# A decoder block on one core: attention products ordered by the probabilities' two parts, and a cast moved to GpSimd

## The chip, the cores and the metric

The kernel runs on one core of a Trainium2 chip. The metric is device time in microseconds of one execution, as the median of several runs. The engines are TensorE (PE, and PEld for its weight loads), VectorE (DVE), ScalarE (ACT), GpSimd (POOL) and SyncE (SP), which here only issues DMAs.

## The reference

One decoder block over 1024 tokens of width 1024, in float32. Dilated attention and a convolution module run side by side on the same normalised input; gates merge them, and a SwiGLU feed-forward layer follows. What matters here is the attention: 24 heads of width 64 in three groups.

```python
DILATED_GROUPS = ((128, 1), (512, 4), (2048, 16))   # window, dilation
...
s = jnp.einsum('brnqhd,brnkhd->brnhqk', qb, kb).astype(jnp.float32) * (Dh ** -0.5) + bias
s = jnp.where(valid[:, None], s, NEG_INF)
lse = jax.nn.logsumexp(s, axis=-1)
p = jnp.exp(s - lse[..., None])
o = jnp.einsum('brnhqk,brnkhd->brnqhd', p, vb.astype(jnp.float32))
...
alpha = jax.nn.softmax(jnp.stack(lses, axis=0), axis=0)
o = jnp.einsum('gbsh,gbshd->bshd', alpha, jnp.stack(outs, axis=0))
```

The other parts are large matrix products, normalisations and a depthwise convolution of 31 taps:

```python
merged = jax.nn.sigmoid(z_ga) * y_attn + jax.nn.sigmoid(z_gc) * y_conv
x = x + rms_norm(merged @ w_mix_out[l], g_post_mix[l])
h = rms_norm(x, g_pre_ffn[l])
x = x + rms_norm(swiglu_ffn(h, w_ffn_in[l], w_ffn_out[l]), g_post_ffn[l])
```

## The kernel before

**Two parts.** An operand of a product is split into a high part, which is the number rounded to TensorE's shorter float32 form, and a low part, which is what the rounding left. A product is then high by high, high by low and low by high. Casts to the high part run on ScalarE as a rule; the subtraction that gives the low part runs on VectorE or GpSimd.

**The order of the work.** All instructions are put out by one program in a fixed order, so each engine's queue is written by hand. The main thread issues the large products. After each group of them it calls `tick`, which runs things that are due by a count of ticks (`later`), and `beat`, which advances the attention: `attention` is a generator, and each `yield` in it is a place where products of the main thread can come between. How many beats fall between the main products is set by a rate (0.42 beside the value projections, 0.8 beside the convolution's output product), so several pauses often follow one another with nothing between. While the attention runs, the main thread computes the value projections (`v`, L954 and L955, with the copies L965 and sums L976), one gate, and the first output products of the convolution (`unit`, L318 to L320, with its splits L190, L191, L1266, L1267 and the result L1613).

**The attention.** It has 96 steps: three groups of heads x 4 pairs of heads x 8 blocks of 128 queries. A pair of heads in a group is a unit of 8 steps. In step `s`:

- `att_s`: the scores of both heads (PE L1067), then their bias and minimum (DVE L1070).
- `att_e`: the exponentials of the step before (ACT L1080).
- a pause; then `added`, what the last finished pair left to do: two additions (`att_o`, DVE L1167).
- `att_t`, four steps behind: one head's probabilities for a pair of blocks are transposed (PE L1105), cast to their high part (`hi`, ACT L1112), and the low part is subtracted (`lo`, DVE L1113).
- a pause; then `att_p`, five steps behind: the values' products with `hi` (PE L1137) and with `lo` (PE L1138). The stationary operand holds, for each block of keys, 64 columns of the values' high part and then 64 of their low part; the product with `lo` uses the first 66 columns only. There are two or three blocks of keys: in the third group two of 128 queries, otherwise a first one of 256 and one or two of 128. There is a pause after the first and after the second block.

After the second head's products the lower 64 rows of the bank are copied out (ACT L1146), and the two additions in the next step add them to the upper 64 rows. When a unit is through, its output goes to memory six ticks later (SP L1173).

**The values.** `value_parts` makes a unit's stationary operand in two halves, in the unit's fourth and fifth step: the cast of the values to their high part (ACT L927) and the subtraction of it (POOL L928). The first products of the unit run in the sixth step. In the second group the even blocks lie in the first half and the odd ones in the second (`place`). In the seventh and eighth step GpSimd copies the next unit's queries within SBUF (`double`, L896 and L897). SyncE loads the next unit's queries, keys and bias (L880, L881, L887, L489) in its first steps, and its values before they are needed (L913).

Of the kernel before, what the change touches and what calls it, by code (L numbers as in the profile page):

```python
# [58 lines left out]
def f(ap):  # L59
    return ap.bitcast(F32)  # L60


class Build:
# [858 lines left out]
    def value_parts(self, x, i):  # L922

        v = self.slot(F32R)
        d = v.rearrange("p (t e c) -> p t e c", t=8, e=2)
        y = x[:, i * H:(i + 1) * H].rearrange("p (t c) -> p t c", t=8)
        self.nc.scalar.copy(d[:, :, 0], y)  # L927
        self.nc.gpsimd.tensor_tensor(d[:, :, 1], y, f(d[:, :, 0]), op=OP.subtract)  # L928
        return v

# [56 lines left out]
    def attention(self):  # L987

        live, s, total = {}, 0, 96
        order = [(g, 2 * hg + i) for hg in range(2) for g in range(3) for i in range(2)]  # L990
        nxt, cur, u, x, V = self.stacks(*order.pop(0)), None, 8, None, None
        for i in range(5):
            self.stack_load(nxt)
        second, doubled = self.stacks(*order.pop(0)), 0

        def there():
            return nxt[1] // 2 * 3 + nxt[0] < self.vn

        while s < total + self.LP:
            if s < total:  # L1000
                if x is None and nxt and there():
                    x = self.values(*nxt[:2])
                if u == 8:
                    while self.normed < 9 or x is None:
                        if second and second[5] < min(5, self.normed - 6):
                            self.stack_load(second)
                        if cur is None and doubled < min(2, self.normed - 5):
                            self.double(nxt, doubled)
                            doubled += 1
                        if x is None and there():  # L1010
                            x = self.values(*nxt[:2])
                        yield 0
                    cur, u, nxt, V = nxt, 0, None, []
                    self.ending = s == total - 8
                live[s] = a = {}
                self.att_s(a, cur, V, u)
                u += 1

                if u in (4, 5):
                    if len(V) < 2:  # L1020
                        V.append(self.value_parts(x, u - 4))
                    if u == 5:
                        x = None
                if u == 6 and cur[0] == 2:
                    self.other_stats(cur)
                if u in (6, 7) and nxt:
                    self.double(nxt, u - 6)
                if u == 8:
                    cur[2] = cur[3] = V = None
                if u == 1:  # L1030
                    if second:
                        nxt, second = second, None
                    elif order:
                        nxt = self.stacks(*order.pop(0))
                if nxt and nxt[5] < 5:
                    self.stack_load(nxt)
            if 0 <= s - 1 < total:
                self.att_e(live[s - 1])
            yield 0
            if self.added:  # L1040
                self.added()
                self.added = None
            if 0 <= s - self.LT < total:
                self.att_t(live, s - self.LT)
                yield 0
            if 0 <= s - self.LP < total:
                yield from self.att_p(live, s - self.LP)
            s += 1
        self.added()
        self.added = None  # L1050

    def att_s(self, a, p, V, u):
# [63 lines left out]
    def att_p(self, live, k):  # L1116


        nc = self.nc
        a, b, hh = live[k & ~1], live[k | 1], k & 1  # L1120
        g, hp, u = a["g"], a["hp"], a["u"]
        if hh == 0:
            a["o"] = self.bank("o")
        ps = a["o"]
        hi, lo = a.pop(("pt", hh))

        if g == 2:
            todo = [(u, 0, 128, 0), (u + 1, 128, 128, 128)]
        else:
            n = 256 + 128 * (len(a["blocks"]) > 1)  # L1130
            todo = [(u, 0, 256, 0)] + [(u - 1, 256, 128, 0)] * (n > 256) + [(u + 1, n, 128, 128)]
        for j, (kb, x, n, q) in enumerate(todo):
            kb = self.place(g, kb)
            v = a["V"][kb // 4]
            c = (kb % 4) * 256 + hh * 128
            o = ps[:, hh * 256 + q:hh * 256 + q + n]
            nc.tensor.matmul(o, v[:, c:c + 128], hi[:, x:x + n], start=j == 0, stop=False, skip_group_check=True)  # L1137
            nc.tensor.matmul(o[0:66], v[:, c:c + 66], lo[:, x:x + n], start=False, stop=j == len(todo) - 1,  # L1138
                             skip_group_check=True)
            if j < 2:  # L1140
                yield 0
        hi = lo = v = None
        if hh == 0:
            return
        low = self.half()
        nc.scalar.copy(low[0:64], ps[64:128])  # L1146
        del live[k - 1], live[k]
        self.added = lambda: self.att_o(a, ps, low)

    def att_o(self, a, ps, low):  # L1150

        nc = self.nc
        g, hp, u = a["g"], a["hp"], a["u"]
        if u == 0:
            self.O = self.ring()

        O = self.O
        e = (8, 2, 128)[g]
        if g == 0:
            d = O.rearrange("p (c m) -> p m c", c=8)[:, u * 16:u * 16 + 32]  # L1160
        elif g == 1:
            d = O.rearrange("p (e c m) -> p c m e", e=2, c=4)[:, u // 2]
        else:
            d = O[:, u * 128:u * 128 + 256].rearrange("p (c m) -> p c m", c=2)
        for h in range(2):
            x, y = (z[0:64, h * 256:(h + 1) * 256].rearrange("p (a e) -> p a e", e=e) for z in (ps, low))
            nc.vector.tensor_tensor(d[h * 64:(h + 1) * 64], x, y, op=OP.add)  # L1167
        a["o"] = None
        if u == 6:

            kept = g == 2 and hp > 1
            if not kept:
                self.later(6, lambda x=self.O: nc.sync.dma_start(self.d_att[g, hp], x))  # L1173
            if g == 2:
                self.merges.append(self.bg(self.merge(hp, a["p"][4], self.O if kept else None)))
            self.O = None
# [885 lines left out]
```

## Time and profile before

| | |
|---|---|
| median of 3 runs | 1698.06 us (1697.9 to 1698.22) |
| profiled execution | 1700.21 us |
| its span, first to last instruction | 1698.4 us |
| granted TensorE clock | 0.999 |
| attention, first scores to last product | 616 to 854 us |
| L927, cast of the values on ScalarE | 24 times, 622 ns mean |
| L928, subtraction on GpSimd | 24 times, 1289 ns mean |

In the rows that follow, an instruction is named by its line, engine and operation, then by what it writes and reads (`b`, `c`, `d` are buffers in SBUF of different sizes, `p` banks in PSUM). Behind a group stand its busy time, the mean duration in ns, and the idle time of its engine just before it with what ended that idle time. A timeline row is start, duration, engine, line, operation, and in brackets the idle time before it. The ends of products are modelled, so the distance from one start to the next says more than their duration.

### The profile page before, as it was taken

Reading aid. Unit: us, or ns where it says so; the run is one execution under the profiler, and the core shown is the slowest. Engines: PE = TensorE matmul, PEld = TensorE weight load, DVE = VectorE, ACT = ScalarE, POOL = GpSimd, SP = SyncE. Lnnn points to the kernel's source line nnn. Section 1 sums busy time; section 2 is a strip of 40 time slices with the busy share of each in tenths; the row PEclk is TensorE's granted clock in tenths of the full one; section 3 lists DMA queues with packets and bytes.
Section 4 is the critical chain, followed back from the end, with each engine's and each line's share of the span. In section 5 each row is a group of like instructions: output and inputs, shape, how many; then the busy total and the mean of one; then the engine's idle time right before and its main releaser. Section 6 shows DMA issues by size and latency. Waiting matters only on the chain.

```text
span 1698.4 us, 23450 instructions
## 1 busy us (share of the span) xinstructions
PE 1675.6 (99%) x8158; PEld 1404.2 (83%) x8158; DVE 1256.8 (74%) x2216; ACT 826.8 (49%) x1622; POOL 492.6 (29%) x369
## 2 busy tenths in 40 slices
PE   8999999999999999999899999999999999999998
PEld 6788888888888889999788888888888888888886
DVE  6789988788999767788885845775665556677686
ACT  6343434343444588888822446543333333354463
POOL 0007777888886254654200300000000000000000
PEclk9999999999999999999999999999999999999999
DMA  4252433355566987779998622132223222494234
GB/s 167 104 186 87 142 131 130 137 191 179 183 173 165 284 270 213 230 224 254 301 275 305 230 87 84 60 129 95 93 93 125 99 93 93 168 377 130 102 130 155
DMA packets 162354, 283.35 MB, mean 167 GB/s; under 512 B 47249, under 2 KB 78732, under 8 KB 162236
## 3 DMA queue, kind: packets, MB, share of 16 engines
q1 hardware_dynamic: 161516, 281.18, 50.8%
q8 instruction: 64, 1.05, 0.3%
q0 software_dynamic: 432, 0.42, 0.1%
q14 instruction: 54, 0.44, 0.1%
q10 hardware_dynamic: 288, 0.27, 0.0%
HBM read 191.10 MB, written 95.42 MB: 169 GB/s over the span
## 4 chain that ended last, share of the span: by engine, by line
PE 90%; DMA 4%; DVE 2%; ACT 1%; issue 1%; POOL 1%; SPq 0%; DVEq 0%; ACTq 0%; POOLq 0%
PE p L334 15%; PE p L335 15%; PE p L336 15%; PE p L1946 12%; PE p L1675 5%; PE p L954 5%; PE p L318 5%; PE p L319 5%; PE p L320 5%; PE p L955 2%; PE p L1067 2%; PE p L1105 1%; DMA b<-dq 1%; PE p L1138 1%; PE p L1137 1%
## 5 line engine op out<-in xcount | busy, mean ns | idle before, releaser
L334 PE MATMUL p<-b,b 128*128 128x512 f32 x1204 | 468.7, 389 | 0.4 <-ACT c L353 0.3
L336 PE MATMUL p<-b,b 128*128 128x512 f32 x1204 | 468.4, 389 | 0.0
L335 PE MATMUL p<-b,b 128*128 128x512 f32 x1204 | 468.4, 389 | 0.0
L334 PEld LDWEIGHTS p<-b,b 128*128 128x128 f32 x1204 | 226.0, 188 | 48.4 <-DVE c L850 1.0
L336 PEld LDWEIGHTS p<-b,b 128*128 128x128 f32 x1204 | 226.0, 188 | 47.1
L335 PEld LDWEIGHTS p<-b,b 128*128 128x128 f32 x1204 | 226.0, 188 | 46.7
L1946 PE MATMUL p<-b,b 128*128 128x512 f32 x924 | 209.6, 389 | 0.0
L1946 PEld LDWEIGHTS p<-b,b 128*128 128x128 f32 x924 | 173.5, 188 | 36.0
L696 DVE SCALAR_TENSOR_TENSOR p<-b,par,p 128x511 f32<-128x511 f32 (+14 forms) x232 | 163.3, 737 | 0.0
L318 PE MATMUL p<-b,b 128*128 128x512 f32 x368 | 147.1, 400 | 0.0
L954 PE MATMUL p<-b,b 128*128 128x512 f32 x384 | 145.2, 410 | 0.0
L320 PE MATMUL p<-b,b 128*128 128x512 f32 x368 | 143.5, 390 | 0.0
L319 PE MATMUL p<-b,b 128*128 128x512 f32 x368 | 143.5, 390 | 0.0
L208 ACT CAST b<-d 128x1024 fp32r<-128x1024 f32 x86 | 90.4, 1051 | 105.1 <-POOL d L229 55.0
L209 POOL TENSOR_TENSOR b<-d,b 128x1024 fp32r<-128x1024 f32 x44 | 106.8, 2428 | 79.8 <-ACT b L208 72.4
L209 DVE TENSOR_TENSOR b<-d,b 128x1024 fp32r<-128x1024 f32 x42 | 51.3, 1221 | 100.8 <-ACT b L208 100.8
L1267 DVE TENSOR_TENSOR b<-b,b 128x512 fp32r<-128x512 f32 x133 | 91.9, 695 | 25.0 <-ACT b L1266 23.2
L955 PE MATMUL p<-b,b 128*128 128x256 f32 x384 | 107.7, 281 | 0.0
L1266 ACT CAST b<-b 128x512 fp32r<-128x512 f32 x133 | 82.1, 619 | 47.7 <-PE p L1946 18.4
L1675 PE MATMUL p<-b,b 128*128 128x512 f32 x384 | 89.4, 391 | 0.0
L208 ACT CAST b<-b 128x1024 fp32r<-128x1024 f32 x47 | 49.4, 1052 | 77.1 <-POOL b L236 37.2
L1080 ACT ACTIVATE c<-c,stat 128x128 f32<-128x128 f32 (+1 forms) x192 | 85.0, 446 | 0.2 <-DVE stat L1070 0.2
(233 smaller groups left out, 2947.7 us busy)
## 6 DMA issues: line engine op xcount, KB each, us to landing
b<-w_in SPq DMA_DIRECT2D x30, 512.0 KB, 4.9
dk<-c SPq DMA_DIRECT2D x48, 256.0 KB, 3.0
dq<-c SPq DMA_DIRECT2D x48, 256.0 KB, 3.6
b<-dq SPq DMA_DIRECT2D x48, 256.0 KB, 3.9
b<-dk SPq DMA_DIRECT2D x48, 256.0 KB, 7.2
b<-w_fi SPq DMA_DIRECT2D x24, 512.0 KB, 4.8
d<-w_in SPq DMA_DIRECT2D x23, 512.0 KB, 3.9
dqS<-c SPq DMA_DIRECT2D x44, 256.0 KB, 2.1
```

Of the source, the lines that this page charges most:

```text
L209: self.wsplit.tensor_tensor(lo, x, f(hi), op=OP.subtract)
L318: nc.tensor.matmul(ps, hi[:, s], a, start=kt == 0, stop=False)
L319: nc.tensor.matmul(ps, hi[:, s], b, start=False, stop=False)
L320: nc.tensor.matmul(ps, lo[:, s], a, start=False, stop=kt == nk - 1)
L334: nc.tensor.matmul(ps, hi[:, s], a, start=first and kt == 0, stop=False, skip_group_check=True)
L335: nc.tensor.matmul(ps, hi[:, s], b, start=False, stop=False, skip_group_check=True)
L336: nc.tensor.matmul(ps, lo[:, s], a, start=False, stop=kt == 3, skip_group_check=True)
L696: nc.vector.scalar_tensor_tensor(A[i][:, j:], src[i][:, :H - j], w[i], A[i][:, j:], op0=OP.mult, op1=OP.add)
L954: nc.tensor.matmul(ps, a, w, start=kt == 0, stop=kt == KT - 1, skip_group_check=True)
L955: nc.tensor.matmul(ps[:, 256:], b, w[:, :256], start=False, stop=kt == KT - 1, skip_group_check=True)
L1675: nc.tensor.matmul(banks[tt][nh], st, wt[:, nh * H:(nh + 1) * H], start=bool(kt == 0 and a), stop=bool(kt == KT - 1 and b))
L1946: nc.tensor.matmul(acc[t], x, y, start=first and e == 0, stop=last and e == 2, skip_group_check=True)
```

## The change

It has three parts.

1. In `att_p` all products with `hi` are issued before all products with `lo`. The two pauses come after the first product with `hi` and after the first with `lo`.
2. `att_o` becomes a generator in two parts. The copy of the lower 64 rows (L1146) is no longer issued right after the products but in the next step, after that step's first pause and ahead of `att_t`. The two additions (L1167) are issued after `att_t` and its pause, so behind the subtraction L1113 in VectorE's queue.
3. In `value_parts` the cast to the high part is issued on GpSimd in place of ScalarE.

```diff
@@ value_parts
-        self.nc.scalar.copy(d[:, :, 0], y)
+        self.nc.gpsimd.tensor_copy(d[:, :, 0], y)
         self.nc.gpsimd.tensor_tensor(d[:, :, 1], y, f(d[:, :, 0]), op=OP.subtract)
@@ attention
             yield 0
-            if self.added:
-                self.added()
-                self.added = None
+            done, self.added = self.added, None
+            if done:
+                next(done)
             if 0 <= s - self.LT < total:
                 self.att_t(live, s - self.LT)
                 yield 0
+            for _ in done or ():
+                pass
+            done = None
             if 0 <= s - self.LP < total:
                 yield from self.att_p(live, s - self.LP)
             s += 1
-        self.added()
+        for _ in self.added:
+            pass
         self.added = None
@@ att_p
-        for j, (kb, x, n, q) in enumerate(todo):
-            kb = self.place(g, kb)
-            v = a["V"][kb // 4]
-            c = (kb % 4) * 256 + hh * 128
-            o = ps[:, hh * 256 + q:hh * 256 + q + n]
-            nc.tensor.matmul(o, v[:, c:c + 128], hi[:, x:x + n], start=j == 0, stop=False, skip_group_check=True)
-            nc.tensor.matmul(o[0:66], v[:, c:c + 66], lo[:, x:x + n], start=False, stop=j == len(todo) - 1,
-                             skip_group_check=True)
-            if j < 2:
-                yield 0
-        hi = lo = v = None
+        for e, (z, cols) in enumerate(((hi, 128), (lo, 66))):
+            for j, (kb, x, n, q) in enumerate(todo):
+                kb = self.place(g, kb)
+                v = a["V"][kb // 4]
+                c = (kb % 4) * 256 + hh * 128
+                o = ps[0:cols, hh * 256 + q:hh * 256 + q + n]
+                nc.tensor.matmul(o, v[:, c:c + cols], z[:, x:x + n], start=e == 0 and j == 0,
+                                 stop=e == 1 and j == len(todo) - 1, skip_group_check=True)
+                if j == 0:
+                    yield 0
+        hi = lo = v = z = None
         if hh == 0:
             return
-        low = self.half()
-        nc.scalar.copy(low[0:64], ps[64:128])
         del live[k - 1], live[k]
-        self.added = lambda: self.att_o(a, ps, low)
+        self.added = self.att_o(a, ps)
 
-    def att_o(self, a, ps, low):
+    def att_o(self, a, ps):
         nc = self.nc
+        low = self.half()
+        nc.scalar.copy(low[0:64], ps[64:128])
+        yield
```

More of the change, by code (lines that the diff above doesn't have):

```diff
@@ L1131, in att_p @@
             todo = [(u, 0, 256, 0)] + [(u - 1, 256, 128, 0)] * (n > 256) + [(u + 1, n, 128, 128)]
-        for j, (kb, x, n, q) in enumerate(todo):
-            kb = self.place(g, kb)
-            v = a["V"][kb // 4]
-            c = (kb % 4) * 256 + hh * 128
-            o = ps[:, hh * 256 + q:hh * 256 + q + n]
-            nc.tensor.matmul(o, v[:, c:c + 128], hi[:, x:x + n], start=j == 0, stop=False, skip_group_check=True)
-            nc.tensor.matmul(o[0:66], v[:, c:c + 66], lo[:, x:x + n], start=False, stop=j == len(todo) - 1,
-                             skip_group_check=True)
-            if j < 2:
-                yield 0
-        hi = lo = v = None
+        for e, (z, cols) in enumerate(((hi, 128), (lo, 66))):
[9 more added lines that the diff above has]
+        hi = lo = v = z = None
         if hh == 0:
             return
+        del live[k - 1], live[k]
+        self.added = self.att_o(a, ps)
+    def att_o(self, a, ps):
+        nc = self.nc
         low = self.half()
         nc.scalar.copy(low[0:64], ps[64:128])
-        del live[k - 1], live[k]
-        self.added = lambda: self.att_o(a, ps, low)
-    def att_o(self, a, ps, low):
-        nc = self.nc
+        yield
         g, hp, u = a["g"], a["hp"], a["u"]
```

## Prediction, made before the changed kernel was run

> **What bounds the kernel now.** I read the page first, then busy time by stretches, then TensorE's waits over the stretch in which the changed lines run (615 to 856 us), then the groups of that stretch, then the timeline at the longest waits.
>
> ```profile
> span 1698.4 us, 23450 instructions
> PE 1675.6 (99%) x8158; PEld 1404.2 (83%) x8158; DVE 1256.8 (74%) x2216; ACT 826.8 (49%) x1622; POOL 492.6 (29%) x369
> ```
>
> TensorE has work in 1675.6 of 1698.4 us, in one fixed order. A change that leaves its products alone can gain only what TensorE stands still or starts late. Where it does so, by stretches (columns: PE, weight loads, VectorE, ScalarE, GpSimd, clock, DMA share, GB/s):
>
> ```profile
> 680.00:700.00 20.00, 19.64 (x150) 18.09 (x148) 15.06 (x53) 17.39 (x57) 11.68 (x14) 1.00 0.81 245
> 800.00:820.00 20.00, 19.08 (x125) 16.23 (x124) 17.34 (x52) 17.90 (x55) 7.84 (x10) 1.00 1.03 288
> 820.00:840.00 20.00, 17.52 (x120) 15.21 (x119) 16.89 (x59) 16.40 (x55) 5.32 (x6) 1.00 1.03 345
> 840.00:860.00 20.00, 17.98 (x103) 14.74 (x102) 14.77 (x41) 8.47 (x26) 0.55 (x1) 1.00 0.92 222
> ```
>
> In the middle of the attention TensorE is nearly full. From 800 on it loses 0.92 + 2.48 + 2.02 = 5.4 us in 60, while VectorE and ScalarE are busy for 82% to 90% of 800 to 840 and the DMA engines are full. TensorE's waits from 610 to 860 (total us, times, longest):
>
> ```profile
> PE p L1138 <- DVE c L1113: 4.9, 7, 1.1
> PE p L1067 <- DVE stat L1070: 2.0, 2, 1.0
> PE p L1137 <- ACT c L1112: 0.8, 1, 0.8
> PE p L1067 <- DMA b<-dk: 0.6, 1, 0.6
> ```
>
> The largest is the low part's product (L1138) waiting for the low part itself (L1113). It is the link that the diff reorders. The groups of 615 to 856 us (busy, mean ns | idle before, ended by):
>
> ```profile
> L1080 ACT ACTIVATE c<-c,stat 128x128 f32<-128x128 f32 (+1 forms) x192 | 85.0, 446 | 0.2 <-DVE stat L1070 0.2
> L1167 DVE TENSOR_TENSOR d<-p,c 64x256 f32<-64x256 f32 x96 | 52.8, 550 | 3.2 <-ACT c L1146 2.5
> L1113 DVE TENSOR_TENSOR c<-p,c 128x384 fp32r<-128x384 f32 (+2 forms) x96 | 52.3, 546 | 26.1 <-ACT c L1112 24.5
> L928 POOL TENSOR_TENSOR b<-b,b 128x512 fp32r<-128x512 f32 x24 | 30.9, 1289 | 70.1 <-ACT b L927 53.0 <-DMA datt<-d 10.6 <-DMA b<-w_co 6.2
> L1138 PEld LDWEIGHTS p<-c,b 128*66 128x66 f32 x216 | 29.8, 138 | 8.3 <-DVE c L1113 7.3
> L896 POOL CAST b<-b 64x512 fp32r<-64x512 f32 x44 | 28.1, 639 | 2.7
> L1146 ACT COPY c<-p 64x512 f32<-64x512 f32 x48 | 28.0, 583 | 13.2 <-PE p L1138 11.8 <-ACT c L1112 0.4
> L927 ACT CAST b<-b 128x512 fp32r<-128x512 f32 x24 | 14.9, 622 | 0.0
> L1267 DVE TENSOR_TENSOR b<-b,b 128x512 fp32r<-128x512 f32 x16 | 12.0, 750 | 4.3 <-ACT b L1266 4.3
> ```
>
> The wait on L1113 is 4.9 us by the products and 7.3 by their weight loads; these are the two ends for what stands to be gained. Now why L1113 is late, at the four longest waits (0.84 to 1.06 us, 3.82 of the 4.9):
>
> ```profile
> 819.33 1.23 DVE L1167 TENSOR_TENSOR d<-p,c 64x256 f32<-64x256 f32 x2
> 820.59 0.42 DVE L1113 TENSOR_TENSOR c<-p,c 128x256 fp32r<-128x256 f32 x1
> 821.07 0.28 PE L1138 MATMUL p<-c,b 128*66 128x128 f32 x1 [1.03 <-DVE c L1113]
> 825.71 0.84 DVE L1167 TENSOR_TENSOR d<-p,c 64x256 f32<-64x256 f32 x2
> 827.06 0.27 PE L1138 MATMUL p<-c,b 128*66 128x128 f32 x1 [0.89 <-DVE c L1113]
> 839.74 0.84 DVE L1167 TENSOR_TENSOR d<-p,c 64x256 f32<-64x256 f32 x2
> 840.62 0.42 DVE L1113 TENSOR_TENSOR c<-p,c 128x256 fp32r<-128x256 f32 x1
> 841.10 0.28 PE L1138 MATMUL p<-c,b 128*66 128x128 f32 x1 [0.84 <-DVE c L1113]
> 847.20 0.75 DVE L1613 SCALAR_TENSOR_TENSOR b<-p,par,b 128x512 f32<-128x512 f32 x1
> 848.33 0.28 PE L1138 MATMUL p<-c,b 128*66 128x128 f32 x1 [1.06 <-DVE c L1113]
> ```
>
> In three of the four the two adds of the finished pair (L1167) run directly ahead of L1113. In the fourth it is the convolution's L1613.
>
> **The change, part by part.**
>
> *The adds go behind L1113.* Both stand in VectorE's queue in the same step; after the change the subtraction comes first and the adds one pause later. At 819.33, 825.71 and 839.74 this brings L1113 forward by 1.23, 0.84 and 0.84 us against waits of 1.03, 0.89 and 0.84, so 2.76 - 0.05 = 2.71 us goes. The fourth stays. That is 2.71 / 3.82 = 71% of these; the same share of the total's ends gives 0.71 x 4.9 = 3.5 and 0.71 x 7.3 = 5.2 us.
>
> *All high products before the low ones.* L1138's first product now comes one or two high products later. Where nothing lies between the pauses that is only about 0.1 us a wait, which takes the 0.05 and a little of the fourth; where conv or value products lie between, more. I take 4.5 us for both edits together (ends 3.5 and 7.3).
>
> *The order's price on TensorE.* No product is added. What can change is which weight load stays hidden:
>
> ```profile
> 707.29 0.39 PE L954 MATMUL p<-b,b 128*128 128x512 f32 x1
> 707.52 0.28 PE L955 MATMUL p<-b,b 128*128 128x256 f32 x1
> 707.87 0.22 PE L1138 MATMUL p<-c,b 128*66 128x128 f32 x1
> 707.93 0.45 PE L954 MATMUL p<-b,b 128*128 128x512 f32 x1
> 708.21 0.28 PE L955 MATMUL p<-b,b 128*128 128x256 f32 x1
> ```
>
> L954 to L955 takes 0.23 us in the first two rows and 0.28 directly behind a short low product: a full load shows by 0.05 us when the product before it has 128 columns to stream. With three blocks, or a first block of 256, I count as many such places as before. With the third group's two blocks of 128 the new order adds one if other work falls into the second pause: 4 head pairs x 8 = 32 times, at most 32 x 0.05 = 1.6 us, at least 0. I take half, 0.8.
>
> *The copy of the lower half (L1146) one pause later.* ScalarE now stands 11.8 us behind it until TensorE has ended L1138, with the exponentials (L1080) queued behind. After the change a pause and the next scores lie between, so nearly all of that idle time goes. ScalarE is off the path in most steps, so I count nothing for it by itself; it is cover for the 4.5. L1146 comes right ahead of L1112 in ScalarE's queue, where it stood ahead of the exponentials, so the sum in front of L1112 is unchanged. If L1146 were the late one, each time costs at most its 0.58.
>
> *The store and loads behind the adds.* The attention's store is issued some ticks after the adds and waits for them; the bias load has had to wait for them too, with all loads of SyncE's queue behind:
>
> ```profile
> SPq L489 <- DVE d L1167: 3.7, 1, 3.7
> SPq L1173 <- DVE d L1167: 1.8, 1, 1.8
> ```
>
> Adds later by one L1113 (0.55) make these at most that much later. In 800 to 840 the DMA share is 1.03 and one load (`dk`) already costs 0.6 us. Ends: 0, and 2 us given back when TensorE runs ahead of full DMA engines. I take 0.4, nearer the one row of 0.6.
>
> *The cast on GpSimd.* ScalarE loses 24 x 0.622 = 14.9 us. GpSimd gets 24 casts; the nearest row, L896, has as many elements per partition on half the partitions at 0.639, and an upper end is the two-input L928 at 1.289. I take 0.65, so 15.6 us. Against that stands 53.0 us in which L928 now waits for ScalarE's cast, which is itself queued behind exponentials and copies. With the cast on its own queue GpSimd can begin as soon as the values are loaded, so V is ready sooner, not later. Queued behind the cast on GpSimd are the value sums (L976) and the doubling casts (L896, L897); they gain the same idle time. At the first unit TensorE's 0.8 us (L1137 <- L1112) goes, since two casts (1.24 us) leave ScalarE ahead of that L1112: 0.8.
>
> What speaks against this cast is sharing between GpSimd and VectorE:
>
> ```profile
> 818.53 0.88 DVE L191 TENSOR_TENSOR b<-b,b 128x512 fp32r<-128x512 f32 x1 [0.72 <-ACT b L190]
> 818.92 0.96 POOL L897 CAST b<-b 64x512 fp32r<-64x512 f32 x1
> 841.37 0.69 DVE L191 TENSOR_TENSOR b<-b,b 128x512 fp32r<-128x512 f32 x1
> ```
>
> Beside each other the two take 0.88 and 0.96, alone 0.69 and 0.64: 0.2 and 0.3 us lost in one meeting. Few VectorE instructions of this kind run here (L1267's 12.0 us is the largest group, 5% of 241 us), so of 24 casts two or three meet one, 0.5 us on VectorE, covered by its idle time. The Trainium skill (GPSIMD Engine Reference, Specifications and Engine selection) says that GpSimd shares its SBUF interfaces with VectorE and contends with VectorE instructions that have two SBUF inputs, while a one-input operation is roughly at line rate; the rows agree in kind. Its advice to keep ordinary elementwise work on VectorE would make this cast a loss; L928's 53.0 us of waiting is why I do not follow it.
>
> *Sum.* 4.5 + 0.8 - 0.8 - 0.4 = 4.1 us. The profiled execution took 1700.21 us, 1.8 more than its span of 1698.4; the gain is inside the span, so 1696.1 for it. The median of the runs, 1698.06, lies 2.15 below that execution: 1694.0 forecast. The ends (3.5 + 0 - 1.6 - 2 and 7.3 + 0.8 - 0 - 0) are about 0 and 8.1, so 1698.1 to 1690.0.
>
> **Rivals.**
> - *The wait comes back as another.* In 800 to 840 VectorE, ScalarE and DMA have 10% to 18% or nothing to spare; if TensorE catches up, the next scores, L1112 or a load is late in its place. Then only what lies ahead of 800 counts: the 0.8 and some of the three shorter waits (4.9 - 3.82 = 1.1): about 1.2 us, 1696.9. For it: the shares. Against: L1113 waits inside one step, the other links have several.
> - *More than forecast.* All of 7.3 and 0.8 go, and the order costs nothing: 1690.0. It needs the fourth wait to go by ScalarE's relief.
> - *VectorE is held by its own queue: slower.* The adds used to fill part of VectorE's 24.5 us of waiting for L1112. Behind L1113 they stand still with it, and the next step's minimum (L1070) behind them. If each of the 10 pairs of 800 to 850 (48 pairs in 241 us) passes one add (0.55) on to TensorE through the scores' banks, that is 5.5 us, less the 0.8: 1702.8. It decides once VectorE has less idle time left per pair of steps than one add: in 800 to 840 it idles 5.8 us over some 8 pairs, 0.7 each, so it is near.
> - *The cast does not help.* In the second group block 1 lies in the second half of the values, so the first products need both halves at once. If GpSimd is busy with other work there, the cast adds its 0.65 to the way of V: 4 head pairs x 0.65 = 2.6 us, less 0.8, and with the reorder worth nothing 1699.9. Against it: 70.1 us of idle time ahead of L928.
>
> **How the numbers follow.** Chances: forecast 0.47 (own range 1691.5 to 1696), wait comes back 0.26, more than forecast 0.13, held by its queue 0.10, cast does not help 0.04. A measurement can tell about 0.2%, 3.4 us, from no change: faster is below 1694.7. That holds for two thirds of the forecast's range (0.33) and for the greater gain (0.13), with 0.02 of the second case: 0.48. Same: the rest of the first (0.14), of the second (0.24) and half of the last (0.02): 0.40. Slower: the third (0.10), and 0.02 in which the last costs more than 3.4 us: 0.12. The range 1689.5 to 1699.5 takes in both ends of the sum; it leaves out the third rival and part of the last.
>
> **What would show it.** Right: TensorE's wait L1138 on L1113 falls from 4.9 to under 2 us; ScalarE's idle time ahead of L1146 from 11.8 to near 0; L1113 runs ahead of the adds; L928's wait on ScalarE is gone and the new cast is 0.6 to 0.75 us; 800 to 860 is 3 us shorter. Wrong: new waits of L1067 on L1070 or on DMA in the same place (second or fourth case), a cast over 1 us, or products by L1137 waiting on GpSimd.

## Result and the profile after

The changed kernel took 1696.08 us (median of 22 runs, 1694.36 to 1698.54) against 1698.28 for the kernel before (22 runs). The ratio is 0.9987, with a 95% interval of 0.9981 to 0.9993: 2.2 us faster, where 4.1 were forecast. The profiled execution took 1696.99 us. The first lines of its page:

```profile
span 1695.1 us, 23430 instructions
PE 1674.8 (99%) x8158; PEld 1404.9 (83%) x8158; DVE 1259.2 (74%) x2216; ACT 816.5 (48%) x1598; POOL 509.5 (30%) x393
```

ScalarE's busy time fell by 10.3 us and GpSimd's rose by 16.9; TensorE does the same work in a span shorter by 3.3. The lines have moved in the listing: the low part's subtraction L1113 is now L1117, the high part's cast L1112 is L1116, both products are L1142, scores and minimum L1071 and L1074, exponentials L1084, transposes L1109, copy L1156, adds L1172. (Each run's listing is its own: where an edit is left out, lines move back.) TensorE's waits from 610 to 860 us:

```profile
PE p L1142 <- DVE c L1117: 3.2, 4, 1.0
PE p L1071 <- DVE stat L1074: 2.0, 2, 1.0
PE p L1071 <- DMA b<-dk: 0.8, 1, 0.8
PE p L1212 <- DVE c L1117: 0.5, 1, 0.5
```

The wait on the low part went from 4.9 to 3.2 us. The first unit's wait on ScalarE (0.8) is gone, and a new one has come, a transpose of the merge (L1212) behind L1117. The stretches from 800 on, with their columns as before:

```profile
800.00:820.00 20.00, 19.02 (x132) 16.74 (x131) 18.12 (x58) 17.17 (x54) 10.53 (x13) 1.00 1.02 300
820.00:840.00 20.00, 19.22 (x131) 16.70 (x131) 18.90 (x69) 18.18 (x59) 4.22 (x4) 1.00 1.04 343
840.00:860.00 20.00, 19.01 (x103) 15.79 (x102) 12.56 (x33) 5.62 (x17) 0.55 (x1) 1.00 1.03 250
```

TensorE now loses 0.98 + 0.78 + 0.99 = 2.75 us there, where it lost 5.4. But a stretch that was full before is not full now; the first row is of the kernel before, the second of the changed one:

```profile
740.00:760.00 20.00, 20.00 (x155) 18.69 (x154) 16.07 (x54) 16.96 (x50) 9.88 (x13) 1.00 0.84 226
```

```profile
740.00:760.00 20.00, 18.57 (x143) 17.17 (x142) 14.73 (x48) 14.36 (x43) 10.30 (x14) 1.00 0.77 211
```

More than half of what was gained behind 800 (2.65 us) is given back here (1.43), in two waits for L1117. Two stretches ahead of it gain 1.2 us (620 to 640 and 680 to 700). Over 600 to 860 TensorE is busy for 253.56 us where it was 251.34: 2.2 us more, which is the gain of the medians, though the two profiled spans differ by 3.3. The groups show what else turned round (615 to 856 us):

```profile
L1084 ACT ACTIVATE c<-c,stat 128x128 f32<-128x128 f32 (+1 forms) x192 | 85.2, 447 | 14.7 <-DVE stat L1074 13.3 <-ACT c L1116 1.0
L1117 DVE TENSOR_TENSOR c<-p,c 128x384 fp32r<-128x384 f32 (+2 forms) x96 | 52.2, 544 | 30.8 <-ACT c L1116 30.4
L928 POOL TENSOR_TENSOR b<-b,b 128x512 fp32r<-128x512 f32 x24 | 31.9, 1330 | 1.9
L1156 ACT COPY c<-p 64x512 f32<-64x512 f32 x48 | 28.0, 584 | 3.5 <-PE p L1142 2.5
L927 POOL CAST b<-b 128x512 fp32r<-128x512 f32 x24 | 16.5, 689 | 12.1 <-DMA b<-dv 12.0
```

The copy's wait on TensorE fell from 11.8 to 2.5 us as expected, and GpSimd's subtraction L928 no longer waits for ScalarE (53.0 us before). The wait has not left GpSimd, though: its sum of the values (L976) now stands 41.1 us behind ScalarE's copy L965, where it was 5.0. Against that the exponentials, which hardly waited for VectorE (0.2), now wait 13.3 us for the minimum, and VectorE waits 30.4 us for the high part where it was 24.5.

### The profile page after: what moved, and what is told of

It reads as the page before. It is cut to its first block, busy times and chain, and to the rows that moved or that the text cites. A ratio compares the mean times of both kernels' runs of the same rounds, so it can differ in the third digit from the quotient of the medians.

```text
span 1695.1 us, 23430 instructions
## 1 busy us (share of the span) xinstructions
PE 1674.8 (99%) x8158; PEld 1404.9 (83%) x8158; DVE 1259.2 (74%) x2216; ACT 816.5 (48%) x1598; POOL 509.5 (30%) x393
## 4 chain that ended last, share of the span: by engine, by line
PE 48%; issue 1%; DVE 1%; ACT 0%; DMA 0%; POOL 0%; DVEq 0%; POOLq 0%
PE p L1951 12%; PE p L334 7%; PE p L335 7%; PE p L336 7%; PE p L1680 5%; PE p L318 3%; PE p L320 3%; PE p L319 3%; PE p L1411 0%; DMA b<-dact 0%; POOL b L928 0%; DVE b L1618 0%; ACT b L1417 0%; DVE b L1240 0%; ACT b L1403 0%
## 5 line engine op out<-in xcount | busy, mean ns | idle before, releaser
L1272 DVE TENSOR_TENSOR b<-b,b 128x512 fp32r<-128x512 f32 x133 | 92.4, 699 | 22.1 <-ACT b L1271 20.2
L1084 ACT ACTIVATE c<-c,stat 128x128 f32<-128x128 f32 (+1 forms) x192 | 85.2, 447 | 14.7 <-DVE stat L1074 13.3
```

## Experiments

Each was timed in turn with the kernel before. Three parts, taken one by one and in pairs, make the first six; the diff above shows each part. The medians come from three sessions, in which the kernel before took 1698.17, 1697.81 and 1698.26 us, so runs are compared by their ratios to it. A ratio of all runs need not equal the ratio of the two medians.

**Order alone** (only the hunk of `att_p`, with copy and adds as before).

> Only the order of the products with the two parts changes; copy, adds and cast stay as in the kernel before. A (the parts add up as the prediction has it): the three waits with the adds ahead of the subtraction stay, each shorter by about 0.1 us, and the weight loads cost 0.8: 0 to 1 us slower, TensorE's wait on the subtraction still 4 to 5 us. B (it is the order that brought the gain, since other work falls between the first high product and the first low one): 2 us faster, that wait under 3 us.

Measured: 1697.69 us, ratio 0.9997 (0.9989 to 1.0006). The wait on the subtraction is 4.0 us, 0.9 less. B falls, on time and wait. A's wait holds at its lower edge; whether the order costs up to 1 us can't be told.

**Later copy and adds alone** (only the hunks of `attention` and `att_o`).

> Only the copy and the adds are issued later; products and cast as before. A: three of the four long waits go, 2.5 to 3.5 us faster, TensorE's wait on the subtraction about 1.5 to 2.2 us. C (the adds, now behind the subtraction, hold the next minimum and so the exponentials, and what is gained in one step is lost in the next): within 1 us of before, ScalarE idle for 10 us and more ahead of the exponentials where it was 0.2.

Measured: 1700.01 us, ratio 1.0014 (1.0005 to 1.0023): slower. VectorE's, ScalarE's and TensorE's waits, a row each:

```profile
DVE c L1117 <- ACT c L1116: 35.6, 49, 1.8
ACT c L1084 <- DVE stat L1074: 10.2, 15, 1.8
PE p L1142 <- DVE c L1117: 4.1, 7, 1.1
```

The wait that the part was to remove is 4.1 of 4.9 us, and VectorE stands 11 us longer ahead of the subtraction. A (the prediction's theory) falls for this part. C holds by its sign: ScalarE waits 10.2 us for the minimum. But the kernel is 2.4 us slower by the ratio, where C had said within 1 us.

**Cast alone** (only the line of `value_parts`).

> Only the cast of the values goes to GpSimd. A: ScalarE is relieved of 14.9 us, the first unit's 0.8 us goes, 0.8 us faster. D (sharing between GpSimd and VectorE): the split of the value weights, 731 ns a piece before, comes to over 900 and small two-input instructions of the merge to over 400, in front of the subtraction: 0.5 to 1.5 us slower.

Measured: 1695.78 us, ratio 0.9989 (0.9980 to 0.9998). One line brings the whole gain:

```profile
PE p L1138 <- DVE c L1113: 2.9, 5, 1.1
DVE c L1113 <- ACT c L1112: 16.5, 33, 1.3
```

VectorE's wait for the high part fell from 24.5 to 16.5 us and TensorE's for the low part from 4.9 to 2.9. A had 0.8 us for this part; it brought 1.9 by the ratio. The split of the value weights (L202) took 740 ns on average against 731, so D falls as the main effect.

**Order and later copy and adds, cast left on ScalarE.**

> Order of the products and the later copy and adds, with the cast left on ScalarE. A: 0.8 us slower than all three parts together, so 1.4 us faster than before. D: the cast costs by sharing, so without it 1 to 2 us faster than with all three, some 3.5 us faster than before, and no wait on the subtraction behind a stretched instruction of the merge.

Measured: 1698.56 us, ratio 1.0006 (0.9997 to 1.0015). Without the cast nothing is left of the gain; D falls for good, and A as well.

**Order and cast.**

> Order of the products and the cast on GpSimd; copy and adds at their old place. E (formed on the first four runs: the cast alone brings the gain, the order some 0.5 us, and the later copy and adds cost about as much as they save): 0.5 us faster than the cast alone, 2.9 us faster than before, and faster than all three parts together. A (the prediction's: the adds behind the subtraction carry the gain): slower than all three together by 2 us or more.

Measured: 1695.27 us, ratio 0.9989 (0.9980 to 0.9997). A falls here too: the adds behind the subtraction are not needed for the gain. E holds as far as can be told; whether this is faster than all three (0.9987) or than the cast alone (0.9989) can't be.

**Later copy and adds, with the cast.**

> The later copy and adds with the cast on GpSimd, products in the old order. E: 1 to 2 us slower than the cast alone, ScalarE idle for 10 us or more ahead of the exponentials. A: faster than the cast alone.

Measured: 1696.64 us, ratio 0.9998 (0.9989 to 1.0007), against 0.9989 for the cast alone. That is 1.5 us slower than the cast alone, about the size of the intervals, and the exponentials wait 15.6 us for the minimum: as E expected, not A.

With the eight corners each part can be read four times, with and without the others:

| part | without others | and the other two, one at a time | with both | mean | in us |
|---|---|---|---|---|---|
| cast | -0.0011 | -0.0008 (order), -0.0016 (late) | -0.0019 | -0.0014 | -2.3 |
| later copy and adds | +0.0014 | +0.0009 (order), +0.0009 (cast) | -0.0002 | +0.0008 | +1.3 |
| order | -0.0003 | -0.0008 (late), 0.0000 (cast) | -0.0011 | -0.0006 | -0.9 |

Each ratio is known to about 0.0009. The mean of four differences is known to some 0.0006 if their errors are independent, so the cast is clear, the later copy and adds just so, and the order is not.

**Is it ScalarE's time or GpSimd's order?** The cast on GpSimd, and at its old place a copy on ScalarE, into a spare buffer that nobody reads:

```diff
+        self.nc.scalar.copy(self.spare.rearrange("p (t c) -> p t c", t=8), y)
         self.nc.gpsimd.tensor_copy(d[:, :, 0], y)
```

> The cast is on GpSimd, and ScalarE makes a copy of the same values at the old place of the cast into a spare buffer that nobody reads. F (the gain is ScalarE's time: without the cast its exponentials and high parts come earlier, so the subtraction does): the gain of the cast is lost, within 0.7 us of before, and TensorE's wait on the subtraction is back at 4 us or more. G (the gain is GpSimd's: its subtraction and what is queued behind it no longer wait for ScalarE): the gain stays, 2 us faster than before, only the first unit's wait may be back.

Measured: 1699.54 us, ratio 1.0010 (1.0001 to 1.0019). Three rows, of ScalarE's group, VectorE's and TensorE's waits (subtraction, high part's cast and product stand two lines later in this listing):

```profile
L928 ACT CAST spare<-b 128x512 bf16<-128x512 f32 x24 | 14.9, 620 | 0.0
DVE c L1115 <- ACT c L1114: 23.2, 39, 1.8
PE p L1140 <- DVE c L1115: 5.3, 8, 1.1
```

The 14.9 us put back on ScalarE bring back VectorE's wait (23.2 against 24.5) and TensorE's (5.3 against 4.9), though GpSimd's subtraction, with 1.9 us of idle time ahead of it, does not wait for ScalarE. G falls and F holds: the gain is ScalarE's time. By the ratio the run is even 1.7 us slower than the kernel before (interval 0.2 to 3.2), where F had said within 0.7; what the rest is, is not shown.

**Copy and adds apart**, with order and cast. First the copy late, with the adds directly behind it:

```diff
             done, self.added = self.added, None
-            if done:
-                next(done)
+            for _ in done or ():
+                pass
             if 0 <= s - self.LT < total:
```

> All three parts, but with the two adds issued directly behind the copy, so ahead of the subtraction as in the kernel before; only the copy is later. J (the adds behind the subtraction are what costs: they stand still while the subtraction waits for its high part, and hold the next minimum): as order and cast together, 0.5 to 1 us faster than all three parts, ScalarE idle ahead of the exponentials for less than 4 us. K (the later copy costs, since it stands on ScalarE directly ahead of the cast of the high part): as all three parts, 1 us slower than order and cast together.

Measured: 1697.68 us, ratio 0.9998 (0.9989 to 1.0006). Then the adds late, with the copy at its old place at the end of `att_p`:

```diff
+        low = self.half()
+        nc.scalar.copy(low[0:64], ps[64:128])
         del live[k - 1], live[k]
-        self.added = self.att_o(a, ps)
+        self.added = self.att_o(a, ps, low)
...
-        low = self.half()
-        nc.scalar.copy(low[0:64], ps[64:128])
         yield
```

> All three parts, but with the copy issued at its old place, right after the products; only the adds are later. J: as all three parts or slower, ScalarE idle for 8 us or more ahead of the exponentials and VectorE 30 us ahead of the subtraction. K: as order and cast together, 1 us faster than all three.

Measured: 1695.94 us, ratio 0.9983 (0.9974 to 0.9992). So K is favoured over J. One row of each: VectorE's adds (L1170 here) behind the copy (L1154) in the first, ScalarE's exponentials in the second:

```profile
DVE d L1170 <- ACT c L1154: 7.3, 15, 1.7
```

```profile
ACT c L1084 <- DVE stat L1074: 2.8, 5, 1.3
```

With the copy late the adds stand 7.3 us waiting for it (2.4 with order and cast). With the adds alone late the exponentials wait only 2.8 us, and 3.4 with the copy alone late. J's other sign did come in the second run, VectorE standing 29.1 us ahead of the subtraction, and yet that run is not slower. It takes both moves to make the 13.3: the copy ahead of the high part's cast on ScalarE, and the adds behind the subtraction on VectorE. The differences between these ratios are about the size of their intervals, so the direction is all that is had. The first profile also holds a wait of 1.9 us on a load and a fall of the clock behind it (below). The clock is not the whole of it: seven of the eleven runs with the copy late have a mean clock of 0.999 or more, and these average 1697.7 us, against 1695.6 for the ten such runs with the adds alone late. What part the load has in the copy's cost was not tried.

**A step more for the low part.** Order and cast, with the transposes three steps behind the scores:

```diff
-    LT, LP = 4, 5
+    LT, LP = 3, 5
```

> Order and cast as in the run before the last, and the transposes three steps behind the scores in place of four, with the products still five behind, so that the low part has two steps until it is used. E: TensorE's waits on the subtraction (2.9 us with the cast alone) go nearly all, 1.5 to 2.5 us faster than order and cast together. H (the low part is late because VectorE and ScalarE are full from 800 on, so that another wait takes the place: exponentials late for the transposes, or buffers): within 1 us of order and cast together.

Measured: 1694.08 us, ratio 0.9977 (0.9968 to 0.9986), so 2.0 us faster than order and cast, as E had it, if by little more than the intervals. No product waits for the low part any more.

> Cast on GpSimd and transposes three steps behind, products in the old order. If a step more for the low part is what gains, the order of the products has nothing left to do: within 0.5 us of the run with three steps and the new order (1694.1). If the order counts by itself, 0.5 to 1 us slower than that.

Measured, for cast and three steps without the order: 1693.21 us, ratio 0.9973 (0.9962 to 0.9983; 7 runs), so no gain of the order shows here. It has the lowest ratio of the study, not to be told from the one before it; it is faster than the kernel before, and than the changed one (0.9987) by little more than the intervals. TensorE's waits:

```profile
PE p L1105 <- DVE c L1113: 2.3, 1, 2.3
PE p L1067 <- DVE stat L1070: 1.3, 2, 1.0
PE p L1406 <- ACT b L1412: 0.2, 1, 0.2
```

What is left of waits is one of 2.3 us and the start. The profile also loses 1.7 us by the clock behind that wait (last section).

> All three parts and transposes three steps behind. J: the adds no longer help, for the low part is not late any more, and they still hold the minimum: 0.5 to 1.5 us slower than the run with three steps, order and cast. A: nothing is held when the low part has a step more, so as fast as that run or faster.

Measured, for all three parts and three steps: 1700.25 us, ratio 1.0008 (0.9999 to 1.0017), 5 to 6 us slower than the two before it by the ratios; 1.7 us of its profile are the clock (last section). ScalarE's waits:

```profile
ACT c L1084 <- DVE stat L1074: 17.2, 21, 3.0
ACT c L1116 <- DVE d L1172: 7.6, 10, 1.0
```

The exponentials have a step less here until the transposes need them, and wait 17.2 us for the minimum; the high part's cast waits 7.6 us for the adds, whose operand lies in the buffer that it wants. A falls. J's expectation held by sign, but the price was more than three times as high as its upper end, and it is copy and adds together that were tried here.

## Why the prediction was right, and where it was not

The sign, the place and the wide range held: 2.2 us of 4.1, in the attention, by a shorter wait on the low part. The measured 1696.08 lies just outside the forecast case's own range (1691.5 to 1696), and the sign set for being right, a wait on the low part under 2 us, was missed with 3.2. The division of the sum did not hold.

- **The adds behind L1113 and the later use of the low part, 4.5 us.** Mis-sized: the two edits without the cast come to 1.0006, some 1 us slower, and with the cast in place they add about 0.3 us of gain (0.9989 to 0.9987); neither is clear of noise. The step that failed is the one from three waits to 71% of the total, with no charge for what the adds' new place does in steps that had no wait. With copy and adds moved, VectorE's wait for the high part is no longer filled; it rose from 24.5 to 35.6 us with this part alone, and the minimum, then the exponentials, are late. The third rival described this, with a chance of 0.10; its price of 5.5 us was too high, 1.3 on average. But by which wait the part costs is not shown: with the adds alone late VectorE waits 29.1 us and nothing is lost (0.9983), and with the copy alone late the exponentials wait only 3.4 us and the gain is gone (0.9998). Which of the two moves costs, and how, stays open.
- **ScalarE "off the path", nothing counted.** This step failed the other way, by 1.5 us. The run that puts a load back shows it: its 14.9 us of casts stood ahead of the high part's casts, on which the subtraction waits, on which TensorE waits. I had quoted 24.5 us of VectorE waiting for L1112 and read it as room for the adds, not as a price of ScalarE's queue. The cast was given 0.8 us and brought 2.3 on average.
- **Two errors cancelled in part.** 4.5 + 0.8 - 0.8 - 0.4 was forecast; the parts' means are +0.9 (order) - 1.3 (later copy and adds) + 2.3 (cast) = 1.9 against 2.2 measured for all. Without the cast 3.3 were forecast, and -0.4 came. That the total came as near as it did is luck.
- **The fourth wait.** It stayed, as said: in the changed kernel a product waits 0.99 us behind the convolution's result at 844.
- **The weight loads, 0.8, and full DMA, 0.4.** The first can't be separated from the order's effect. The wait on `dk` went from 0.6 to 0.8 in the profile, 0.2 instead of 0.4. In the other profiles it lies anywhere from none (four runs, later copy and adds alone among them) to 1.9 us (copy late, adds ahead of the subtraction), so the way by the adds that the prediction gave is not shown.
- **GpSimd's cast.** 0.65 was taken; 689 ns on average, 612 in the median. Sharing was put at nothing on the path, and that was too little in one place, though it is not the cast that shares there. VectorE, GpSimd and TensorE in the changed kernel at 751 us:

```profile
750.34 1.29 POOL L928 TENSOR_TENSOR b<-b,b 128x512 fp32r<-128x512 f32 x1
750.61 0.25 DVE L1205 RECIPROCAL mrg<-mrg 128x16 f32<-128x16 f32 x1
750.90 0.83 DVE L1206 TENSOR_TENSOR mrg<-mrg 128x48 f32<-128x48 f32 x1
752.30 0.68 DVE L1117 TENSOR_TENSOR c<-p,c 128x512 fp32r<-128x512 f32 x1
753.03 0.33 PE L1142 MATMUL p<-c,b 128*66 128x256 f32 x1 [0.97 <-DVE c L1117]
```

L1206 (L1201 in the kernel before) takes 248 to 252 ns there. Here it takes 0.83 us and ends 0.1 us after GpSimd's L928 does; the subtraction is behind it, and TensorE waits. So some 0.58 of this wait's 0.97 us is sharing (0.83 - 0.25, an estimate). The Trainium skill (GPSIMD Engine Reference, Specifications) names VectorE instructions with two SBUF inputs as those that contend, and this row agrees. But L928 ran on GpSimd before as well, and the same meeting comes without the cast, with later copy and adds alone:

```profile
751.73 1.28 POOL L928 TENSOR_TENSOR b<-b,b 128x512 fp32r<-128x512 f32 x1 [2.98 <-PE p L1142]
751.83 1.28 DVE L1206 TENSOR_TENSOR mrg<-mrg 128x48 f32<-128x48 f32 x1
```

With the cast alone it takes 1.38 us there, and the longest wait of a product in that stretch is 0.29 us. So the meeting is one of timing, and it costs where the subtraction has no room left. The split of the value weights tells the same, before and after the change:

```profile
L202 DVE TENSOR_TENSOR b<-b,b 128x512 fp32r<-128x512 f32 x12 | 8.8, 731 | 10.8 <-ACT b L201 9.8 <-POOL b L897 0.7
L202 DVE TENSOR_TENSOR b<-b,b 128x512 fp32r<-128x512 f32 x12 | 11.5, 956 | 9.6 <-ACT b L201 9.2 <-POOL b L928 0.2
```

This lengthening, on which D was built, comes with the later copy and adds and not with the cast: 896 and 860 ns in the two runs that have the moves without the cast, 740 with the cast alone. It is not the whole price of the moves either: with the adds alone late it is 890 ns, and nothing is lost.

- **The chain that remained.** At 815 us the first rival is at work:

```profile
814.26 1.26 DVE L1172 TENSOR_TENSOR d<-p,c 64x256 f32<-64x256 f32 x2
815.55 0.29 DVE L1074 CUSTOM_DVE_ANT_0 c<-p,c 128x128 f32<-128x128 f32 x1
815.89 0.40 ACT L1084 ACTIVATE c<-c,stat 128x128 f32<-128x128 f32 x1 [0.71 <-DVE stat L1074]
815.98 0.73 DVE L1272 TENSOR_TENSOR b<-b,b 128x512 fp32r<-128x512 f32 x1
816.63 0.41 DVE L1117 TENSOR_TENSOR c<-p,c 128x256 fp32r<-128x256 f32 x1
817.10 0.27 PE L1142 MATMUL p<-c,b 128*66 128x128 f32 x1 [0.98 <-DVE c L1117]
```

The adds, now late, hold the minimum; that holds ScalarE's exponentials; a split of the convolution (L1272) comes in between, and the subtraction is late after all.

## What to carry to other kernels

When a late instruction is found behind others in a queue, ask first what feeds it from another engine: an engine that is busy for 80% to 90% of a stage can be on the path of whatever waits for it, even if hardly a wait of the bounding engine names it. Here taking 0.6 us at a time off it was worth more than a better order. Work that fills another instruction's wait is free where it stands and may cost where it is moved to; charge a reorder for the steps that had no wait as well. Where a link has one step of slack and its neighbours have several, a step moved between them can do what reorders do not: here (4, 5 to 3, 5) it took away every product's wait on the low part, but together with the later copy and adds it came out 5 us slower.

## What the runs showed of the hardware

Three of the fourteen profiles show waits of TensorE that cost more than their length. In the run with the copy late TensorE waited 1.86 us for `dk` at 821 us, and the granted clock (third column from the right) fell afterwards:

```profile
821.00:823.00 2.00, 0.75 (x7) 0.57 (x5) 0.93 (x4) 1.07 (x2) 0.00 (x0) 1.00 1.05 273
823.00:825.00 2.00, 1.38 (x5) 1.22 (x6) 1.99 (x8) 1.15 (x5) 0.00 (x0) 0.70 1.04 412
825.00:827.00 2.00, 2.00 (x9) 1.70 (x8) 1.48 (x7) 0.88 (x3) 0.00 (x0) 0.50 1.07 387
827.00:829.00 2.00, 2.00 (x14) 1.68 (x13) 1.76 (x7) 1.95 (x8) 0.76 (x2) 0.95 1.03 391
```

Over these 6 us the clock lost 0.6 + 1.0 + 0.1 = 1.7 us, nearly the wait again. The other two are the cast with three steps, behind its wait of 2.3 us, and all three parts with three steps, where no single wait is long: TensorE's weight loads waited 0.65, 0.31, 0.60 and 0.36 us between 817.8 and 820.3. That run:

```profile
819.00:821.00 2.00, 1.51 (x6) 0.89 (x7) 1.97 (x8) 1.52 (x7) 0.54 (x1) 0.94 1.05 236
821.00:823.00 2.00, 2.00 (x10) 1.90 (x9) 1.61 (x8) 1.95 (x7) 0.00 (x0) 0.50 0.99 310
823.00:825.00 2.00, 2.00 (x10) 1.58 (x10) 1.96 (x6) 1.47 (x6) 0.00 (x0) 0.70 1.04 392
```

Read in quarters of a microsecond, the clock of all three stands at 0.50 for 3.4 us (823.8 to 827.2, 816.0 to 819.4, 820.8 to 824.2) and at 1.00 on both sides, so each loses 1.7 us, not much less than the whole change gained. A wait of 1.44 us at the same place (later copy and adds, with the cast) left the clock at 1.00, and so did one of 2.2 us (three steps, order and cast); why one wait is followed by it and another is not, these runs do not settle.
